# A decoder block on one core: x loaded right behind c, the first transfers in a fixed order, silu on c's row, and matmuls on zeros while TensorE waits

## The chip, the cores and the metric

The kernel runs on one core of a Trainium2 chip. The metric is the device time of one execution in microseconds (us), given as the median of the runs shown. Engines are named as in the profile: PE is TensorE's matmul, PEld its weight load, DVE is VectorE, ACT is ScalarE, POOL is GpSimd, and SP (SPq in the trace) is SyncE, which issues the DMAs.

## What is computed

The reference is one decoder block on x of shape (1, 1024, 1024) with a conditioning vector c of 1024 numbers. Cut to what the change touches:

```python
c_act = silu(c)
cond = c_act @ ada_w + ada_b          # six rows of 1024: shift1, scale1, gate1, shift2, ...
h = rmsnorm(x, norm1_g) * (1 + scale1) + shift1
z = h @ w_in + b_in                   # u, v, val, gate: 512 columns each
y_a = spatial_gating_mixer(gelu(u), gelu(v), ...)
y_b = conformer_conv_mixer(val, gate, ...)   # val * sigmoid(gate), causal conv of 31 taps, norm, silu
x = x + gate1 * (concat(rmsnorm(y_a), rmsnorm(y_b)) @ w_out)
h2 = rmsnorm(x, norm2_g) * (1 + scale2) + shift2
x = x + gate2 * ((silu(h2 @ w_g) * (h2 @ w_up)) @ w_ffn_out)
return rmsnorm(x) * norm_f_g * (1 + scale_f) + shift_f
```

## The kernel before

x lies transposed in `xs`, eight tiles of 128 features by 1024 tokens, and the block works on the tokens in two halves of 512. Every matrix product is done in three matmuls (`mm3`, L623 to L627, and `product`, L945): each operand is split into a high part (ACT, a copy to the reduced type) and a low part (DVE or POOL, a subtraction), and high times high (L625), low times high (L626) and high times low (L627) are summed in a bank.

The stage that the change touches is the first one.

- c's row is loaded (L540), then x's first half in eight transfers of 256 KB (L545) and `colt`, the small parameter columns (L546). Only "behind c" is laid down for them, not what may come between.
- L558 to L561: two matmuls spread c's row over 128 partitions (one per half of the row), and ACT's silu on each result gives `cact`. A one-column sqrt behind them (L564) makes ACT load the table for sqrt early.
- The first norm is `rstd` (L653): for each of the eight tiles, ACT squares it (L663) and four narrow matmuls (128x32 by 128x128) sum the squares over the partitions (L670); then sqrt (L673, ACT), reciprocal (L674, DVE), four wide matmuls that spread the result over the partitions (L676), and with `copy=True` a copy from the bank into `r_n` (L682, ACT).
- The loop over the eight tiles k (L740 to L754): two rows of the conditioning weights of 512 KB each are loaded into `ypad` (L576; four buffers, so two tiles k deep), DVE multiplies each with `cact` and sums (L581), which gives the column of scale1 and of shift1 for this k. ACT finishes these (L744, L745). The weights `wk` of this k are loaded (512 KB, L603) and split (L608 on ACT, L609 on DVE). x is multiplied by the norm (L747, DVE), modulated (L749 gives the high part of h, L750 the full value, both ACT), and L751 (DVE) gives h's low part. Then 24 matmuls of 128x512: eight units of `wk` (four groups j, value and gate each), three matmuls each, into eight banks, so all of PSUM is taken in this loop.
- Behind the loop come `glu` (L693), the projection of u (`pu`), the second half's norm, the convolution (`conv_pair`, L867, on ACT, POOL and for the most part DVE), the mixer and so on; the feed-forward stage fills the second half of the time.

What is written in program order is not the order on the engines. At the end `fix_order` (L473) takes all instructions, plans the whole program three times over with its own table of costs (`duration`, L126, and the class `Clock`, L317), forwards (`forward`, L376) and backwards (`backward`, L433), keeps the best plan, and lays each engine's order down by that plan, SP's included. The pairs in `edges` go into the plan as "later behind earlier" (L209); a context `issue_after` (L498) makes such pairs on one engine. Until now an edge between two DMAs meant "behind the end of the earlier". Tiles of one tag take their buffers in program order (`Slots`, L243); the tag `raw` has four buffers, which c's row, `wk` and most later weights share.

Of the kernel before, what the change touches and what calls it, by code (L numbers as in the profile page):

```python
# [13 lines left out]
P = 128  # L14
# [20 lines left out]
N_POOL_TAPS = (6, 6)  # L35

# [135 lines left out]
class Graph:  # L172


    def __init__(self, instructions, edges, stacked, reusing):
# [32 lines left out]
        by_name = {s.ins.name: s for s in self.steps}  # L208
        for later, earlier in edges:  # L209
            by_name[later].before.add(by_name[earlier].n)  # L210
# [165 lines left out]
def forward(g, rank):  # L376
# [25 lines left out]
    for _ in range(count):  # L402
# [21 lines left out]
        for n in s.after:  # L424
            need[n] -= 1
            same = g.steps[n].engine == e and not s.dma
            at[n] = max(at[n], (clock.free[e] if e == "PE" else end) if same else end + SIGNAL[e])
            if not need[n]:
                arrive(n)
# [3 lines left out]
def backward(g, rank, follows):  # L433
# [16 lines left out]
    for _ in range(count):  # L450
# [13 lines left out]
        for n in before[s.n]:  # L464
            need[n] -= 1
            other = g.steps[n].engine
            at[n] = max(at[n], begin + s.issue - (s.finish - s.issue) if other == e == "PE" else end + SIGNAL[other])
# [22 lines left out]
def block_kernel(ctx: ExitStack, tc: tile.TileContext, xT, c, ada, cols, vbias, bs, wsp,  # L490
# [52 lines left out]
    with issue_after(c_load):  # L543
        for k in range(KD):
            nc.sync.dma_start(xs[k][:, hs(0)], xT[k, :, hs(0)])  # L545
        nc.sync.dma_start(colt, cols)  # L546

# [8 lines left out]

    cact = const.tile([P, D], F32, name="cact")
    for h in range(2):  # L558
        cb = cv_bank(f"c{h}")
        PE.matmul(cb, ones[0:1].broadcast_to([1, P]), c_row[0:1, hs(h)], start=True, stop=True)  # L560
        silu = A.activation(cact[:, hs(h)], cb, AF.Silu).ins  # L561
# [39 lines left out]
    def weights(src, name, lo_eng, tag="w"):  # L601
        raw = sb.tile([P, 1024], F32, tag="raw", name=f"raw_{name}", bufs=N_RAW)
        nc.sync.dma_start(raw, src)  # L603
# [4 lines left out]
        A.activation(hi, raw, AF.Copy)  # L608
        lo_eng.tensor_tensor(lo, raw, hi.bitcast(F32), op=ALU.subtract)  # L609
# [123 lines left out]
    r1a_bank, r1a = rstd(x_half(0), D, "n1_0", (1,) * 8, None, True)  # L733
    h1 = [[None] * KD, [None] * KD]
    alloc = [cv_bank] * 2 + [gn_bank] * 2 + [mm_bank] * 3 + [nrm_bank]
    acc = {(j, vg): alloc[2 * j + vg](f"p{j}_{vg}") for j in range(4) for vg in range(2)}
    gain = const.tile([P, KD], F32, name="gain")
    V.scalar_tensor_tensor(gain, bcol(SCALE1, 0, KD), 1.0, colt[:, _OFF["norm1_g"]:_OFF["norm1_g"] + KD],
                           op0=ALU.add, op1=ALU.mult)
    for k in range(KD):  # L740
        for m, g in ((SCALE1, 0), (SHIFT1, 1)):
            ada_cols(m * 8 + k, dst=ypad[(2 * k + g) % 4][:, HALO:HALO + D])
        w_k = weights(wk[k], f"k{k}", V)
# [5 lines left out]
        A.activation(h[:, 0, :], t, AF.Identity, bias=ccol(SHIFT1, k), scale=ccol(SCALE1, k))  # L749
        A.activation(t, t, AF.Identity, bias=ccol(SHIFT1, k), scale=ccol(SCALE1, k))  # L750
        V.tensor_tensor(h[:, 1, :], t, h[:, 0, :].bitcast(F32), op=ALU.subtract)  # L751
        for j in range(4):
            for vg in range(2):
                mm3(acc[j, vg], unit(w_k, 4 * vg + j), full(h), k == 0, k == KD - 1)  # L754
# [688 lines left out]
```

## Time and profile before

| | |
|---|---|
| time, median of 3 runs | 990.24 us (989.9 to 991.04) |
| span of the profiled execution | 988.3 us; its whole time is not listed apart |
| instructions | 13193 |
| DVE, share of the span | 862.3 us, 87% |
| ACT, POOL | 474.2 us (48%), 399.5 us (40%) |
| bytes moved by DMA | 184.08 MB, mean 186 GB/s |

A profile row gives busy times of one execution. PE's share counts matmuls that overlap in the pipeline: one of 128x512 is shown with about 390 ns, and the next begins some 227 ns behind it at full clock. So the starts, not the durations, tell how fast PE works. Rows of the timeline give start, duration, engine, line, operation, output and inputs, and in brackets how long the engine had been idle and what ended that. Rows of the chain give start, duration, engine, tile and line of the work that the last instruction can be followed back to. Rows by stretch give, for each engine, busy time and instructions, then the granted clock, the DMA engines' busy share and GB/s.

### The profile page before, as it was taken

Reading aid. Unit: us, or ns where it says so; the run is one execution under the profiler, and the core shown is the slowest. Engines: PE = TensorE matmul, PEld = TensorE weight load, DVE = VectorE, ACT = ScalarE, POOL = GpSimd, SP = SyncE. Lnnn points to the kernel's source line nnn. Section 1 sums busy time; section 2 is a strip of 40 time slices with the busy share of each in tenths; the row PEclk is TensorE's granted clock in tenths of the full one; section 3 lists DMA queues with packets and bytes.
Section 4 is the critical chain, followed back from the end, with each engine's and each line's share of the span. In section 5 each row is a group of like instructions: output and inputs, shape, how many; then the busy total and the mean of one; then the engine's idle time right before and its main releaser. Section 6 shows DMA issues by size and latency. Waiting matters only on the chain.

```text
span 988.3 us, 13193 instructions
## 1 busy us (share of the span) xinstructions
PE 961.0 (97%) x4645; PEld 774.3 (78%) x4645; DVE 862.3 (87%) x1197; ACT 474.2 (48%) x750; POOL 399.5 (40%) x232
## 2 busy tenths in 40 slices
PE   6999999999999999999999999999999999999994
PEld 3887777778878778888888888888888887888873
DVE  4989999879999654799999999999779989869946
ACT  6778467553473563564323333323337437236416
POOL 0058879665554211574454544554443100000121
PEclk9999999999999999999999999999999999999997
DMA  9982451434465524864677677767659928315104
GB/s 328 333 308 83 139 173 53 170 107 128 149 227 178 160 80 166 261 230 149 222 239 243 218 240 254 256 220 228 221 178 298 325 83 260 126 36 179 33 1 170
DMA packets 72515, 184.08 MB, mean 186 GB/s; under 512 B 8065, under 2 KB 8321, under 8 KB 72450
## 3 DMA queue, kind: packets, MB, share of 16 engines
q1 hardware_dynamic: 72450, 183.25, 55.7%
q8 instruction: 36, 0.59, 0.3%
q14 instruction: 29, 0.24, 0.1%
HBM read 142.06 MB, written 41.16 MB: 185 GB/s over the span
## 4 chain that ended last, share of the span: by engine, by line
PE 81%; DVE 10%; ACT 4%; issue 2%; DMA 1%; POOL 1%; SPq 0%; ACTq 0%; DVEq 0%; POOLq 0%
PE B L950 28%; PE C L950 16%; PE ah L950 11%; DVE cv L888 4%; PE A L950 3%; PE po L625 3%; PE po L626 3%; PE po L627 3%; PE p L627 3%; PE p L625 3%; PE p L626 3%; PE pm L829 1%; PE gn L923 1%; DVE w_f L943 1%; DVE x L581 1%
## 5 line engine op out<-in xcount | busy, mean ns | idle before, releaser
L950 PE MATMUL B<-h,w_f 128*128 128x512 f32 x816 | 190.0, 390 | 1.1 <-DVE x L1169 1.0
L950 PEld LDWEIGHTS B<-h,w_f 128*128 128x128 f32 x816 | 152.8, 188 | 34.3 <-DVE x L1169 2.2
L888 DVE SCALAR_TENSOR_TENSOR cv<-ypad,colt,cv 128x512 f32<-128x512 f32 x216 | 146.3, 746 | 0.1
L950 PE MATMUL B<-fa,w_d 128*128 128x512 f32 x528 | 125.3, 390 | 0.5 <-DVE x L1302 0.5
L950 PE MATMUL C<-h,w_f 128*128 128x512 f32 x528 | 123.6, 389 | 0.0
L950 PEld LDWEIGHTS B<-fa,w_d 128*128 128x128 f32 x528 | 98.7, 188 | 21.9 <-DVE x L1302 1.0
L950 PEld LDWEIGHTS C<-h,w_f 128*128 128x128 f32 x528 | 99.1, 188 | 20.6
L950 PE MATMUL ah<-h,wh_a 128*128 128x512 f32 x320 | 100.8, 394 | 0.5 <-ACT sg L695 0.5
L1231 POOL TENSOR_TENSOR sq_nf<-sq_nf,sq_nf 128x512 f32<-128x512 f32 x9 | 12.4, 1374 | 178.3 <-ACT sq_nf L1226 178.3
L942 ACT ACTIVATE w_d<-raw_d 128x512 fp32r<-128x512 f32 (+1 forms) x72 | 42.0, 593 | 82.0 <-PE B L950 34.6
L609 POOL TENSOR_TENSOR wl_a<-raw_a,wh_a 128x1024 fp32r<-128x1024 f32 x20 | 49.3, 2464 | 72.3 <-ACT wh_a L608 62.2
L942 ACT ACTIVATE w_f<-raw_f 128x512 fp32r<-128x512 f32 x68 | 42.3, 628 | 74.3 <-PE B L950 41.6
L1192 POOL TENSOR_TENSOR x<-x,up 128x512 f32<-128x512 f32 x20 | 35.1, 1753 | 105.5 <-ACT x L1191 105.5
L950 PEld LDWEIGHTS ah<-h,wh_a 128*128 128x128 f32 x320 | 59.8, 188 | 14.9 <-issue 1.4
L943 DVE TENSOR_TENSOR w_f<-raw_f,w_f 128x512 fp32r<-128x512 f32 x68 | 65.6, 970 | 3.5 <-ACT w_f L942 3.4
L950 PE MATMUL C<-fa,w_d 128*128 128x512 f32 (+1 forms) x273 | 64.4, 384 | 0.2 <-DVE x L1302 0.2
L950 PE MATMUL ah<-h,wl_a 128*128 128x512 f32 x160 | 62.8, 394 | 0.0
L950 PEld LDWEIGHTS C<-fa,w_d 128*128 128x128 f32 x273 | 49.9, 188 | 10.8 <-issue 0.6
L1302 DVE SCALAR_TENSOR_TENSOR x<-B,cond,x 128x512 f32<-128x512 f32 x48 | 35.6, 743 | 23.2 <-PE B L950 23.2
L943 DVE TENSOR_TENSOR fa<-a,fa 128x512 fp32r<-128x512 f32 x77 | 53.3, 732 | 1.5 <-ACT fa L942 1.5
L942 ACT ACTIVATE fa<-a 128x512 fp32r<-128x512 f32 x77 | 46.2, 626 | 8.3 <-DMA a<-acts 5.2
L943 DVE TENSOR_TENSOR w_d<-raw_d,w_d 128x512 fp32r<-128x512 f32 (+1 forms) x72 | 46.6, 658 | 0.0
(236 smaller groups left out, 2115.0 us busy)
## 6 DMA issues: line engine op xcount, KB each, us to landing
acts<-x SPq DMA_DIRECT2D x77, 256.0 KB, 2.9
a<-acts SPq DMA_DIRECT2D x77, 256.0 KB, 4.3
raw_f<-wf SPq DMA_DIRECT2D x32, 512.0 KB, 4.5
ada<-ada SPq DMA_DIRECT2D x24, 512.0 KB, 3.4
x<-ada SPq DMA_DIRECT2D x24, 512.0 KB, 3.6
raw_a<-wf SPq DMA_DIRECT2D x20, 512.0 KB, 3.8
ahead<-ahead SPq DMA_DIRECT2D x40, 256.0 KB, 3.1
ypad<-ada SPq DMA_DIRECT2D x16, 512.0 KB, 5.3
```

The lines of the kernel that those rows point to most:

```text
L581: V.scalar_tensor_tensor(raw, raw, 1.0, cact, op0=ALU.mult, op1=ALU.mult, accum_out=cond[:, j:j + 1])
L609: lo_eng.tensor_tensor(lo, raw, hi.bitcast(F32), op=ALU.subtract)
L625: PE.matmul(acc, shi, mhi, start=start, stop=False)
L626: PE.matmul(acc, slo, mhi, start=False, stop=False)
L627: PE.matmul(acc, shi, mlo, start=False, stop=stop)
L888: V.scalar_tensor_tensor(accs[j], src, wc, accs[j], op0=ALU.mult, op1=ALU.add)
L942: A.activation(dst[:, 0, :], src, AF.Copy)
L943: lo_eng.tensor_tensor(dst[:, 1, :], src, dst[:, 0, :].bitcast(F32), op=ALU.subtract)
L950: last_mm = PE.matmul(bank[:, cols], s, m[:, cols], start=first and p == 0 and i == 0, stop=p == n - 1 and i == 2, skip_group_check=True)
L1192: G.tensor_tensor(g0, g0, up0, op=ALU.mult)
L1231: G.tensor_tensor(sums[half], sums[half], t, op=ALU.add)
L1302: V.scalar_tensor_tensor(xs[k][:, part], bank[:, cols], ccol(GATE2, k), xs[k][:, part], op0=ALU.mult, op1=ALU.add)
```

## The change

1. **Order of the first transfers.** `first_loads` holds the first ten DMAs (c, eight of x, `colt`), and edges put each behind the one before. `in_turn` appends the loads of the loop over k: scale row, shift row, weights, for k = 0 to 7. So nothing of the loop is issued ahead of x. `wk` of k = 0 is loaded and split in two parts of 512 columns.
2. **The planner.** An edge between two DMAs without another reason to wait is now a "turn": the later may be issued 0.44 us (the plan's figure) behind the earlier's issue, no longer behind its end.
3. **silu on c's row.** One silu of 1 x 1024 on ACT ahead of the two matmuls, and two copies from the banks to `cact` on DVE.
4. **The first norm** is written out in `first_rstd`: tiles 1 and 3 and half of tile 7 are squared on DVE. r's copy goes behind the high part of the first h. Of k = 0, the product with x reads the bank as before.
5. **Matmuls on zeros.** A tile `idle` of zeros (128x512, bf16) is multiplied into the bank of group 3's value, which the loop's first real matmul there overwrites: 3 ahead of c, 1 behind the sums of each of tiles 0 to 6, 4 behind tile 7's, 8 behind the matmuls that spread r; 22 in all. The banks of the loop are allocated when first used, this one at once.

```diff
+IDLE = (3, 1, 4, 8)
...
         for later, earlier in edges:
-            by_name[later].before.add(by_name[earlier].n)
+            a, b = by_name[later], by_name[earlier]
+            if a.dma and b.dma and b.n not in a.before:
+                self.turns.add((b.n, a.n))
+            a.before.add(b.n)
...
+            if (s.n, n) in g.turns:
+                at[n] = max(at[n], t + DMA_ISSUE)
...
+    first_loads = [i for i in nc.cur_bb.bb.instructions if "DMACopy" in type(i).__name__]
...
+    idle = front.tile([P, H], BF16, tag="vn", name="idle", bufs=4)
+    V.memset(idle, 0.0)
+    def keep_busy(n, after=None):
+        for _ in range(n):
+            ins = PE.matmul(idle_bank, idle[:, 0:P], idle, start=True, stop=True).ins
+            if after is not None:
+                edges.append((ins.name, after.name))
...
+    c_banks_0 = [cv_bank(f"c{h}") for h in range(2)]
+    idle_bank = first_bank(3, 0)
+    keep_busy(IDLE[0])
+    silu = A.activation(c_row[0:1, :], c_row[0:1, :], AF.Silu).ins
     for h in range(2):
-        cb = cv_bank(f"c{h}")
-        PE.matmul(cb, ones[0:1].broadcast_to([1, P]), c_row[0:1, hs(h)], start=True, stop=True)
-        silu = A.activation(cact[:, hs(h)], cb, AF.Silu).ins
+        PE.matmul(c_banks_0[h], ones[0:1].broadcast_to([1, P]), c_row[0:1, hs(h)], start=True, stop=True)
+        V.tensor_scalar(cact[:, hs(h)], c_banks_0[h], 1.0, None, op0=ALU.mult)
...
+        cuts = [slice(i * 1024 // parts, (i + 1) * 1024 // parts) for i in range(parts)]
+        for cut in cuts:
+            nc.sync.dma_start(raw[:, cut], src[:, cut])
...
+        for cut in cuts:
+            A.activation(hi[:, cut], raw[:, cut], AF.Copy)
+            lo_eng.tensor_tensor(lo[:, cut], raw[:, cut], hi[:, cut].bitcast(F32), op=ALU.subtract)
...
-    r1a_bank, r1a = rstd(x_half(0), D, "n1_0", (1,) * 8, None, True)
+    def first_rstd():
+        bank = nrm_bank("ssq_n1_0")
+        for k in range(KD):
+            src = xs[k][:, hs(0)]
+            t = tmp(f"sq_n1_0_{k}")
+            if k in (1, 3):
+                V.tensor_tensor(t, src, src, op=ALU.mult)
+            elif k == KD - 1:
+                A.activation(t[:, 0:256], src[:, 0:256], AF.Square)
+                V.tensor_tensor(t[:, 256:H], src[:, 256:H], src[:, 256:H], op=ALU.mult)
+            else:
+                A.activation(t, src, AF.Square)
+            for q in range(4):
+                mm = PE.matmul(bank[q * 32:(q + 1) * 32, 0:P], ones.broadcast_to([P, 32]),
+                               t[:, q * P:(q + 1) * P], start=k == 0, stop=k == KD - 1).ins
+            keep_busy(IDLE[2] if k == KD - 1 else IDLE[1], mm)
+        rt = sb.tile([P, P], F32, tag="rt", name="rt_n1_0", bufs=2)
+        A.activation(rt, bank[:, 0:P], AF.Sqrt, bias=epst, scale=1.0 / D)
+        V.reciprocal(rt, rt)
+        for q in range(4):
+            mm = PE.matmul(bank[:, q * P:(q + 1) * P], col("sel_tok", q).broadcast_to([P, P]),
+                           rt, start=True, stop=True).ins
+        keep_busy(IDLE[3], mm)
+        return bank
...
+    def in_turn(n):
+        for i in nc.cur_bb.bb.instructions[n:]:
+            if "DMACopy" in type(i).__name__:
+                edges.append((i.name, first_loads[-1].name))
+                first_loads.append(i)
+    for a, b in zip(first_loads[1:], first_loads):
+        edges.append((a.name, b.name))
     for k in range(KD):
-        for m, g in ((SCALE1, 0), (SHIFT1, 1)):
-            ada_cols(m * 8 + k, dst=ypad[(2 * k + g) % 4][:, HALO:HALO + D])
-        w_k = weights(wk[k], f"k{k}", V)
+        n_before = len(nc.cur_bb.bb.instructions)
+        ada_cols(SCALE1 * 8 + k, dst=ypad[2 * k % 4][:, HALO:HALO + D])
+        ada_cols(SHIFT1 * 8 + k, dst=ypad[(2 * k + 1) % 4][:, HALO:HALO + D])
+        w_k = weights(wk[k], f"k{k}", V, parts=2 if k == 0 else 1)
+        in_turn(n_before)
...
-        A.activation(h[:, 0, :], t, AF.Identity, bias=ccol(SHIFT1, k), scale=ccol(SCALE1, k))
+        h_hi = A.activation(h[:, 0, :], t, AF.Identity, bias=ccol(SHIFT1, k), scale=ccol(SCALE1, k)).ins
+        if k == 0:
+            with issue_after(h_hi):
+                A.activation(r1a, r1a_bank, AF.Copy)
```

More of the change, by code (lines that the diff above doesn't have):

```diff
@@ L466, in backward @@
             other = g.steps[n].engine
+            if (n, s.n) in g.turns:
+                at[n] = max(at[n], begin + DMA_ISSUE)
+                if not need[n]:
+                    heapq.heappush(waiting[other], (at[n], n))
+                continue
             at[n] = max(at[n], begin + s.issue - (s.finish - s.issue) if other == e == "PE" else end + SIGNAL[other])
@@ L753, in block_kernel @@
             for vg in range(2):
[L754 removed]
+                mm3(first_bank(j, vg), unit(w_k, 4 * vg + j), full(h), k == 0, k == KD - 1)
     first_phase_loaded = ada_dma[SHIFT1 * 8 + KD - 1].ins
```

19 lines of the change are left out of this document (12 added, 7 removed).

## The prediction

> **What bounds the kernel now.** I read the page first: its head, the engines' shares and the chain that ended last.
>
> ```profile
> span 988.3 us, 13193 instructions
> ...
> PE 961.0 (97%) x4645; PEld 774.3 (78%) x4645; DVE 862.3 (87%) x1197; ACT 474.2 (48%) x750; POOL 399.5 (40%) x232
> ...
> PE 81%; DVE 10%; ACT 4%; issue 2%; DMA 1%; POOL 1%; SPq 0%; ACTq 0%; DVEq 0%; POOLq 0%
> ```
>
> TensorE carries the end: 97% busy, 81% of the chain. An average hides where the missing time lies, so next the busy times by stretch (after the engine's own time: PE, PEld, DVE, ACT, POOL).
>
> ```profile
> 0.00:20.00 20.00, 10.96 (x77) 5.06 (x78) 6.93 (x13) 12.21 (x21) 0.49 (x8) 1.00 0.90 334
> ```
>
> ```profile
> 20.00:65.00 45.00, 45.00 (x190) 36.95 (x189) 41.07 (x57) 30.78 (x46) 7.99 (x3) 1.00 0.92 315
> 65.00:100.00 35.00, 34.37 (x205) 26.66 (x204) 33.64 (x49) 30.08 (x47) 27.78 (x20) 1.00 0.42 147
> 100.00:160.00 60.00, 59.90 (x338) 47.15 (x337) 59.69 (x93) 37.03 (x58) 50.94 (x26) 1.00 0.42 134
> ...
> 400.00:700.00 300.00, 298.97 (x1343) 246.30 (x1335) 295.80 (x362) 112.08 (x183) 149.99 (x88) 1.00 0.71 231
> ```
>
> PE misses 9 us of the first 20, and almost nothing later: from 20 to 160 it is idle for 0.7 us, from 400 to 700 for 1.0. So what PE wins in the first 20 us reaches the end unless something makes it wait later. The timeline of those 20 us shows the chain that holds it up:
>
> ```profile
> 1.22 0.82 SPq L576 DMA_DIRECT2D ypad<-ada  x2
> 2.09 4.54 SPq L545 DMA_DIRECT2D x<-xT  x8
> ...
> 2.40 3.75 PE L560 MATMUL c<-c_row,ones 1*128 1x512 f32 x4 [2.40 <-DMA c_row<-c]
> ...
> 6.98 0.63 ACT L663 ACTIVATE sq_n<-x 128x512 f32<-128x512 f32 x1 [0.20 <-DMA x<-xT]
> 7.63 1.28 ACT L564 ACT_TABLE_LOAD   x1
> ...
> 8.93 0.20 ACT L564 ACTIVATE warm<-epst 128x1 f32<-128x1 f32 x1
> 9.03 3.92 ACT L663 ACTIVATE sq_n<-x 128x512 f32<-128x512 f32 x7
> ...
> 9.70 3.96 PE L670 MATMUL ssq_n<-sq_n,ones 128*32 128x128 f32 x56 [1.38 <-ACT sq_n L663]
> ...
> 13.72 0.37 ACT L673 ACTIVATE rt_n<-ssq_n,epst 128x128 f32<-128x128 f32 x1 [0.22 <-PE ssq_n L670]
> 13.99 1.05 ACT L608 ACTIVATE wh_k<-raw_k 128x1024 fp32r<-128x1024 f32 x1
> 14.12 0.95 DVE L674 RECIPROCAL rt_n<-rt_n 128x128 f32<-128x128 f32 x1 [1.36 <-ACT rt_n L673]
> ...
> 15.13 2.08 PE L676 MATMUL ssq_n<-rt_n,colt 128*128 128x128 f32 x8 [1.48 <-DVE rt_n L674]
> 17.25 0.60 ACT L682 ACTIVATE r_n<-ssq_n 128x512 f32<-128x512 f32 x1 [2.21 <-PE ssq_n L676]
> 17.88 0.69 DVE L747 TENSOR_TENSOR t_h<-x,ssq_n 128x512 f32<-128x512 f32 x1 [1.58 <-ACT r_n L682]
> 18.60 0.81 ACT L749 ACTIVATE h<-t_h,cond 128x512 fp32r<-128x512 f32 x1 [0.76 <-DVE t_h L747]
> ...
> 19.47 0.80 PE L625 MATMUL p<-h,wh_k 128*128 128x512 f32 x1 [2.26 <-ACT h L749]
> ```
>
> Two conditioning rows (1 MB) go ahead of x, so x's first tile lands at 6.98; ACT loads the sqrt table and squares until 12.95; sums, sqrt, reciprocal, the spreading matmuls, r's copy, product and modulation follow one another, and the first real matmul starts at 19.47. Then it is slow:
>
> ```profile
> 24.10 0.43 PE p L626
> ...
> 24.83 0.23 PE p L625
> ```
>
> ```profile
> 65.48 0.39 PE L625 MATMUL pu<-h,wh_u 128*128 128x512 f32 x1
> ...
> 86.88 1.16 PE L676 MATMUL ssq_n<-rt_n,colt 128*128 128x128 f32 x8
> ```
>
> Up to 24.1 one matmul takes 0.43 us, from 24.83 on 0.23 (65.48 is where the loop's 192 matmuls are over; at 0.2267 they need 43.5). (65.48 - 24.83) / 0.2267 is 179 matmuls, so 13 ran in the slow 5.36 us, which at the fast pitch are 2.95: the slow start costs **2.4 us**. The granted clock reads 1.00 there, so the pitch is the evidence. The same eight spreading matmuls took 2.08 us at 15.13 and 1.16 at 86.88: PE was at half pace then, too, although it had been busy with the narrow sums.
>
> **The change part by part.** *Loads.* Stretches of the DMA engines:
>
> ```profile
> 2.70:5.40 2.70, 2.70 (x4) 0.83 (x3) 0.00 (x0) 0.60 (x1) 0.00 (x0) 1.00 0.98 362
> 5.40:11.60 6.20, 3.30 (x41) 1.01 (x40) 2.38 (x4) 5.19 (x9) 0.00 (x0) 1.00 1.01 347
> 14.00:20.00 6.00, 2.61 (x9) 2.28 (x10) 4.29 (x6) 3.00 (x5) 0.00 (x0) 1.00 1.02 409
> ```
>
> ```profile
> SPq L546 <- DMA x<-xT: 0.3, 1, 0.3
> ```
>
> Before 5.4 the 1 MB of conditioning passes, then x's 2.1 MB at 347 GB/s in 6.05 us; tile 0's bytes are through at 6.15 and it lands at 6.96, 0.8 later. With x first the same starts at 2.7: tile 0 lands at 4.2, tile 7 at 9.6. Behind it `colt` (138.5 KB, 0.4), then 512 KB each at 409 GB/s, 1.28 us: the scale row lands at 11.2, the shift row at 12.5, the two parts of `wk` (256 KB, 0.76 each at x's rate) at 13.3 and 14.05, k = 1's three at 15.3, 16.6 and 17.9. SP issues in this order; it already waits for earlier landings (row above), and its queue holds nothing else that is due then. The conditioning lands 4 us later than before; what covers this is that it is wanted only with r.
>
> *silu and squares.* c is there at 2.4. silu on 1x1024 is bounded by ACT's rows of that width (`wh_k`, 1.05) and of half of it (0.63); I take 1.05, the nearest: 3.45. The sqrt table (1.28) and the one-column sqrt (0.2) end at 4.95, when tile 0 has been there for 0.7. ACT then has five and a half squares of 0.56 and DVE two and a half of about 0.69 (its 128x512 rows), all faster than x lands (0.76 a tile). So the last half square ends 0.4 behind tile 7: 10.0, against 12.95. The two copies to `cact` on DVE (0.61 to 0.75 each, nearest its product row's 0.69) lie where DVE is idle before, in front of the first product at 12; the zero tile's fill too, whatever it costs below that.
>
> *Chain.* Sums 0.7 behind the last square, as before (12.95 to 13.66): 10.75. sqrt 0.4: 11.15. Reciprocal: 12.1. Spreading 1.16 to 2.08: 13.3 to 14.25. r's copy (0.63) leaves the path; ACT does it behind h, and r is next wanted by k = 1's product four us later. Now **DVE is late next**. Its rows:
>
> ```profile
> 18.48 1.22 DVE L581 SCALAR_TENSOR_TENSOR ypad<-ypad,cact 128x1024 f32<-128x1024 f32 x1
> 19.63 1.22 DVE L581 SCALAR_TENSOR_TENSOR ypad<-ypad,cact 128x1024 f32<-128x1024 f32 x1
> ...
> 28.89 0.68 DVE L751 TENSOR_TENSOR h<-t_h,h 128x512 fp32r<-128x512 f32 x1
> ...
> 33.52 0.68 DVE L751 TENSOR_TENSOR h<-t_h,h 128x512 fp32r<-128x512 f32 x1
> ```
>
> The conditioning products (a new one can start every 1.15) run from 12.1 to 14.4, then the product with x to 15.1, h to 15.95, with signals of 0.03 to 0.06 each step: the first real matmul at **16.2**. If DVE takes the product with x straight behind the spreading, 14.9; that is the lower end. From there DVE needs 4.63 us for one k (28.89 to 33.52), PE 5.44, so PE is fed: k = 1's h is ready at about 20.7, PE is through k = 0 at 21.6. A landing 0.9 later than worked out would show as a wait there.
>
> *Zeros.* No bf16 matmul is in the trace; between nothing and twice the loop's pitch, I take that pitch, 0.23 fast and 0.43 slow, the nearest row of that width. Ahead of c and between the sums the zeros delay nothing if PE is fast by then; the last eight fill 1.8 of the 2.9 us between the spreading and 16.2 (at twice the pitch 3.6, and the start is 16.9). If PE is slow they cost, see the second rival.
>
> When does PE get fast? It is busy with few breaks from 3.45: c's matmuls 3.75, then sums and zeros. The trace before has 5.0 us of unbroken 128x512 matmuls ahead of the change of pitch, and it shows narrow sums (9.7 to 13.7) that brought none. The Trainium skill, TensorE: Matmul & The Clock Gate, Part 1, has half rate as the default and full rate after one busy window of about 3.4 us that runs freely. By that rule a busy time from 3.45 opens the clock by 10.3 at the latest; that the narrow sums did not open it speaks against counting every matmul as busy. By the rule the start stays 16.2 (16.8 at worst), by the strict reading of the rows it is the second rival.
>
> *Sum.* Start 19.47 - 16.2 = 3.3, pace 2.4: **5.7 us**. The loop ends at 59.7 instead of 65.48. DVE's added 3.2 us (squares, copies) lie in its 13 idle us before 20. The span would be 982.6. The median of the runs is 990.24, 1.9 above the one profiled span; taken off there: **984.5**.
>
> All engines' orders are planned anew, so every later wait may shift by some tenths in either direction. I put that at nothing, within 1 us each way.
>
> **The rivals.** *A, DVE in the convolution holds the time.* The chain runs on DVE before the mixer's matmuls at 145.6:
>
> ```profile
> 95.46 13.91 DVE cv L888 x22
> ...
> 145.63 1.97 PE gn L923 x32
> ```
>
> From 20 to 160 DVE is busy 134.4 of 140. Work up to 160 is then 6.9 + 134.4 + 3.2 = 144.5; 4.6 of it is over at 12.1 (fills, copies, squares, gain, reciprocal). The other 139.9 with the same 5.6 of waits end at 157.6: only 2.4 earlier, time 987.8. Without the waits it would be 8.0 earlier. For A: that chain. Against: part of those waits are for PE's loop, which ends earlier, and PE has other matmuls at hand.
>
> *B, the zeros do not open the clock.* At half pace c's matmuls end at 7.2, eight sums of 0.56 (3.96 / 7) and seven zeros of 0.43 at 14.7, the reciprocal at 16.1, the spreading at 18.2. If the clock opens half-way through the last eight zeros, they end at 20.8. Loop end 20.8 + 43.5 = 64.3, gain 1.2: 989.0. The change would then not do what it says; the zeros would cost what the early x brings.
>
> *C, slower: DVE overruns in the feed-forward stage.* From 400 to 700 DVE has 4.2 us left of 300, and PE lives on its splits. DVE's time there depends on what lies beside it:
>
> ```profile
> L581 DVE SCALAR_TENSOR_TENSOR x<-x,cact x24: 1209/1215/2322, 477.9 to 691.6; 128x1024 f32<-128x1024 f32 x24
> ```
>
> ```profile
> L581 DVE SCALAR_TENSOR_TENSOR x<-x,cact 128x1024 f32<-128x1024 f32 x24 | 36.0, 1502 | 0.0
> ```
>
> The same product takes 1.21 to 2.32 us, on average 1.50. If the new order put all 24 at 2.32, DVE would need 19.7 more; 4.2 is free, PE loses 15.5, less 5.7: 1000.0. It decides from 9.9 us more DVE time on (parity); at three quarters, 14.8, the time is 995.1. Against it: only the first stage's costs change, and the order there need not.
>
> **How the numbers follow.** Forecast 0.58 (own range 983 to 986), A 0.15, B 0.15, C 0.12. This kernel's measurement can tell about 0.2%, 2 us, from no change. Faster: the forecast, A and a little of B, 0.77; same: the rest of B, 0.12; slower: C, 0.11. The low end is the start at 14.9 (gain 7.0) with some tenths of luck, 982.8; the high end takes in A and B, 989.2; C is left out.
>
> **What would show it.** Right: tile 0's square starts near 5, the last ends near 10, the first real matmul of the loop starts near 16 with pitch 0.23 at once, `pu` begins near 59.7, and PE has under 2 us of new waits behind it. Wrong: the spreading matmuls still take 2.08 and the zeros stand between h and the first real matmul (B); `pu` early but the mixer's matmuls near 145 not earlier by more than 3 (A); DVE's products above 1.5 us in the feed-forward stage and PE waiting for w_f (C). If tile 7 lands later than 10.5, my rate for x was wrong, and the start moves with it.

## The result, and the profile after

The changed kernel takes **992.58 us** (median of 20 runs, 989.08 to 995.05), the kernel before in the same comparison 990.4 (20 runs, 989.25 to 991.8): a ratio of 1.0022, 95% interval 1.0014 to 1.003. It is 2.2 us slower where 5.7 us less were forecast, and lies 3.4 us above the predicted range. Its profiled execution took 994.9 (span 993.2), so it stands 2.3 above the median: what is read from it is a slow example of its kind.

The head of its page, the shares, and the chain that ended last:

```profile
span 993.2 us, 13233 instructions
...
PE 968.5 (98%) x4667; PEld 775.4 (78%) x4667; DVE 860.1 (87%) x1204; ACT 473.6 (48%) x748; POOL 392.9 (40%) x232
...
PE 73%; DVE 15%; DMA 5%; issue 2%; ACT 2%; SPq 1%; POOL 1%; ACTq 0%; DVEq 0%; POOLq 0%
```

TensorE's share of the chain fell from 81% to 73%, DVE's rose from 10% to 15% and the DMAs' from 1% to 5%: other things than PE now end waits. The start of its timeline:

```profile
4.00 0.63 ACT L782 ACTIVATE sq_n<-x 128x512 f32<-128x512 f32 x1 [0.61 <-DMA x<-xT]
...
9.32 2.08 ACT L782 ACTIVATE sq_n<-x 128x512 f32<-128x512 f32 x3 [2.65 <-DMA x<-xT]
...
11.43 0.42 ACT L779 ACTIVATE sq_n<-x 128x256 f32<-128x256 f32 x1
...
12.03 0.61 PE L584 MATMUL p<-idle 128*128 128x512 bf16 x1
12.57 0.66 PE L784 MATMUL ssq_n<-sq_n,ones 128*32 128x128 f32 x8
13.16 3.17 PE L584 MATMUL p<-idle 128*128 128x512 bf16 x7
...
13.69 0.95 DVE L789 RECIPROCAL rt_n<-rt_n 128x128 f32<-128x128 f32 x1 [1.74 <-ACT rt_n L788]
14.56 1.16 DVE L615 SCALAR_TENSOR_TENSOR ypad<-ypad,cact 128x1024 f32<-128x1024 f32 x1
...
15.65 1.22 DVE L615 SCALAR_TENSOR_TENSOR ypad<-ypad,cact 128x1024 f32<-128x1024 f32 x1
...
16.12 1.10 PE L791 MATMUL ssq_n<-rt_n,colt 128*128 128x128 f32 x8
...
17.06 2.54 PE L584 MATMUL p<-idle 128*128 128x512 bf16 x11
...
17.26 0.69 DVE L820 TENSOR_TENSOR t_h<-x,ssq_n 128x512 f32<-128x512 f32 x1 [0.38 <-PE ssq_n L791]
...
18.04 0.81 ACT L822 ACTIVATE h<-t_h,cond 128x512 fp32r<-128x512 f32 x1 [0.31 <-DVE t_h L820]
...
19.24 0.58 PE L662 MATMUL p<-h,wh_k 128*128 128x512 f32 x1
```

x's first tile is there at 4.00, close to the 4.2 worked out, but the fifth only at 9.32, and the last half tile is squared at 11.43. The program has eleven zero matmuls behind the tiles' sums, one for each of seven tiles and four behind the last. One of the eleven came to stand ahead of the last sums (12.03) and seven in one heap at 13.16, ahead of the matmuls that spread r: the reciprocal is done at 14.64, the spreading starts at 16.12. Eleven more, the remaining three and the last eight, fill PE up to 19.2, while h is ready at 18.85. The first real matmul starts at 19.24, 0.23 earlier than before.

By stretch (PE, PEld, DVE, ACT, POOL; granted clock, DMA share, GB/s):

```profile
3.00:11.40 8.40, 7.55 (x52) 2.39 (x52) 2.58 (x4) 4.92 (x8) 0.00 (x0) 1.00 0.90 315
...
20.00:65.00 45.00, 43.72 (x193) 35.86 (x192) 39.00 (x57) 30.67 (x48) 5.45 (x2) 1.00 0.86 287
65.00:100.00 35.00, 32.85 (x194) 25.93 (x193) 30.15 (x45) 29.47 (x43) 28.62 (x19) 0.95 0.57 195
80.00:85.00 5.00, 5.00 (x35) 3.48 (x28) 4.64 (x8) 4.44 (x7) 5.00 (x4) 0.66 0.54 169
```

PE's waits from 58 to 90 and from 400 to 700, each for the kernel before and then after (total, times, longest):

```profile
PE ssq_n L670 <- ACT sq_n L663: 0.4, 1, 0.4
```

```profile
PE ssq_n L707 <- ACT sq_n L700: 2.1, 1, 2.1
PE pu L662 <- ACT sg L732: 1.3, 1, 1.3
```

```profile
PE B L950 <- DVE x L1169: 1.0, 2, 0.7
```

```profile
PE B L1026 <- DVE x L1245: 2.9, 3, 1.5
```

The loop runs at full pace from its first matmul, and its last one starts at 62.8 (before: 65.3). So 2.5 us were won there. Then PE waits 1.3 us for the sigmoids that free the banks for `pu` and 2.1 us for the squares of the second half's norm, and behind this second wait the clock falls: 0.66 over 80 to 85 is 5.00 x 0.34 / 0.5 = 3.4 us at half pace, 1.7 us lost. With 3.0 us more of waits and 1.7 of clock, the 2.5 us have become a loss of some 2.2 by 85. The feed-forward stage adds 1.9 us of waits for `x` (2.9 against 1.0).

### The profile page after: what moved, and what is told of

Its sections match the earlier page's. It is cut to its first block, busy times and chain, and to the rows that moved or that the text cites. A ratio compares the mean times of both kernels' runs of the same rounds, so it can differ in the third digit from the quotient of the medians.

```text
span 993.2 us, 13233 instructions
## 1 busy us (share of the span) xinstructions
PE 968.5 (98%) x4667; PEld 775.4 (78%) x4667; DVE 860.1 (87%) x1204; ACT 473.6 (48%) x748; POOL 392.9 (40%) x232
## 4 chain that ended last, share of the span: by engine, by line
PE 73%; DVE 15%; DMA 5%; issue 2%; ACT 2%; SPq 1%; POOL 1%; ACTq 0%; DVEq 0%; POOLq 0%
PE B L1026 23%; PE C L1026 13%; PE ah L1026 11%; PE po L662 3%; PE po L663 3%; PE po L664 3%; PE A L1026 3%; DVE cv L964 2%; DVE w_f L1019 2%; PE p L662 2%; PE p L663 2%; PE p L664 2%; DVE x L615 1%; PE v L662 1%; DMA a<-acts 1%
## 5 line engine op out<-in xcount | busy, mean ns | idle before, releaser
L1026 PE MATMUL ah<-h,wl_a 128*128 128x512 f32 x160 | 62.8, 394 | 0.0
L1019 DVE TENSOR_TENSOR w_d<-raw_d,w_d 128x512 fp32r<-128x512 f32 (+1 forms) x72 | 48.6, 685 | 0.4 <-ACT w_d L1018 0.4
```

What stands on the lines that cost most here:

```text
L1019: lo_eng.tensor_tensor(dst[:, 1, :], src, dst[:, 0, :].bitcast(F32), op=ALU.subtract)
L1026: last_mm = PE.matmul(bank[:, cols], s, m[:, cols], start=first and p == 0 and i == 0, stop=p == n - 1 and i == 2, skip_group_check=True)
```

## The experiments

Each kernel was timed beside the kernel before, whose median there was 989.96 to 990.67; the ratio is to that. Three landmarks are read from each profile: where PE starts the projection of u (`pu`) and DVE the glu, both behind the first loop, and where PE starts the mixer's first `gn` matmul. Kernels called "pinned" have, behind the plan's time 53.5, the kernel before's own order on every engine. So their `gn` stands in the same place of the same order as in the kernel before, and its time tells what was won or lost up to there.

| kernel | median (n) | ratio, 95% interval | `pu` | glu | `gn` |
|---|---|---|---|---|---|
| before, profiled execution | | | 65.48 | 63.11 | 138.76 |
| the changed kernel | 992.58 (20) | 1.0022, 1.0014 to 1.003 | 64.44 | 63.27 | |
| after_again | 993.25 (7) | 1.0033, 1.0023 to 1.0044 | 63.41 | 62.24 | |
| p1_before_order | 992.78 (7) | 1.0028, 1.0017 to 1.0039 | 65.03 | 66.27 | 140.03 |
| p2_ffn_before_order | 990.36 (12) | 0.9993, 0.9981 to 1.0006 | 62.46 | 61.29 | |
| p3_before_ffn_after_order | 991.82 (9) | 1.0018, 1.0009 to 1.0028 | 64.94 | 62.57 | 138.23 |
| q1_bank | 991.27 (11) | 1.0009, 1.0 to 1.0018 | 64.08 | 67.20 | 142.78 |
| q2_no_zeros | 991.42 (11) | 1.0005, 0.9996 to 1.0015 | 64.77 | 65.04 | 140.76 |
| q3_zeros_in_place | 989.63 (11) | 0.9993, 0.9984 to 1.0002 | 64.42 | 64.71 | 138.36 |
| q4_before_bank_first | 990.25 (11) | 1.0, 0.9992 to 1.0009 | 66.11 | 63.73 | 139.41 |
| r1_rows | 990.14 (11) | 0.9997, 0.9988 to 1.0006 | 64.64 | 64.91 | 138.27 |
| r2_rows_ahead | 989.26 (12) | 0.9993, 0.9984 to 1.0003 | 64.48 | 63.92 | 140.05 |
| r3_x_first | 989.86 (11) | 1.0, 0.9991 to 1.0009 | 64.79 | 62.42 | 138.07 |
| r4_before_rows | 990.73 (11) | 1.0, 0.9992 to 1.0009 | 64.90 | 62.52 | 138.19 |
| s1_x_early | 993.58 (5) | 1.0032, 1.002 to 1.0044 | 66.17 | 67.94 | 142.17 |
| s2_before_x_early | 991.47 (12) | 1.0014, 1.0004 to 1.0023 | 65.62 | 65.89 | 139.26 |
| s3_more_dve | 990.87 (11) | 1.0005, 0.9996 to 1.0013 | 64.80 | 64.62 | 138.13 |
| s5_product_behind_glu | 992.78 (11) | 1.0028, 1.0019 to 1.0037 | 65.77 | 66.40 | 141.38 |
| t1_zeros_alone | 991.12 (12) | 1.001, 1.0 to 1.0021 | 67.82 | 65.45 | 141.06 |
| t2_zeros_x_first | 991.16 (12) | 1.0001, 0.9992 to 1.001 | 65.64 | 65.89 | 139.36 |

The landmarks belong to one execution each and shift by a microsecond or two from one to the next (q4, which computes just as the kernel before, has its `gn` 0.65 later). So a verdict rests on the ratio, and the landmarks say where to look.

### Is it the new order of the engines?

The first theory: the engines' orders, planned anew, give back what the start wins. p1 takes the changed kernel with the old orders from 53.5 on, p2 only from 338 on (the feed-forward stage), and p3 puts the new order of that stage into the kernel before. after_again is the changed kernel once more.

```diff
+    pin(best[1], g.steps)
     for steps in best[1].values():
         for earlier
```

> The changed kernel once more, as the control on the same chip and for a second profile. Every theory: 1.002 times the kernel before. Theory 1 (the re-made order of the rest costs): the second profile too shows the loop over k done 2 to 3 us earlier than before, and 3 to 4 us lost again between 460 and 640 us, where PE waits for DVE. Theory 2 (the first stage's own side effects cost, and what follows is only shifted in time): the loss between 460 and 640 differs from profile to profile by more than 2 us.

> The changed kernel, but everything behind the first half or so of the loop over k (the plan's time 53.5) keeps the order that the kernel before has on every engine. Theory 1 (the re-made order of the rest costs): faster than before, by the 2.5 us that the loop ends earlier in the first profile, less the 1.3 us that the first projection of u waits for the bank that the zeros took: 1 to 2.5 us faster, ratio 0.9975 to 0.999. Theory 2 (the first stage's own side effects, the bank and the clock, cost): still slower than before by 1 us or more, ratio over 1.001.

> The changed kernel, but from the plan's time 338 on (the last of the block ahead of the feed-forward stage, and that stage) every engine keeps the order of the kernel before. Theory 1: the 3 to 4 us that were lost in the feed-forward stage come back, so the time is 2 to 3.5 us under the changed kernel's, ratio to before 0.999 to 1.0015. Theory 2: no change against the changed kernel, ratio 1.002.

> The kernel before, with nothing of the change, but from the plan's time 338 on with the order that the changed kernel has on every engine. Theory 1: the loss comes with this order alone, 2 to 4 us slower than before, ratio 1.002 to 1.004. Theory 2: the order makes no difference, ratio 0.9995 to 1.0005.

The changed kernel came out slower again. With the feed-forward stage's old order (p2) it is level with the kernel before: 2.9 us are that order's by the medians (993.25 - 990.36), 4.0 by the ratios. Put into the kernel before, the same order alone costs 1.9 us (991.82 against 989.96, whose ratio's interval lies above 1). PE's waits for `x` from 400 to 700, in p2 and in p3:

```profile
PE B L1141 <- DVE x L1360: 0.5, 1, 0.5
```

```profile
PE B L1065 <- DVE x L1284: 1.8, 3, 1.0
```

So the order of that stage is shown to cost 2 to 4 us. But it is not all: p2 still has nothing of the 5.7 us, and p1, whose orders are old from 53.5 on, missed its expectation altogether. Its place of loss is the one that the profile after showed. PE's waits from 58 to 90, then DVE's rows there, then PE's stretch 60 to 70 in p1:

```profile
PE pu L829 <- ACT sg L899: 2.3, 1, 2.3
PE ssq_n L874 <- ACT sq_n L867: 0.4, 1, 0.4
```

```profile
65.11 1.23 DVE L782 SCALAR_TENSOR_TENSOR ada<-ada,cact 128x1024 f32<-128x1024 f32 x1 [3.25 <-DMA ada<-ada]
...
66.27 2.72 DVE L901 SCALAR_TENSOR_TENSOR ypad<-p,colt,sg 128x512 f32<-128x512 f32 x4
```

```profile
60.00:70.00 10.00, 7.67 (x27) 5.82 (x27) 6.72 (x11) 7.42 (x11) 4.81 (x3) 0.83 0.79 283
```

The glu stands on DVE behind a conditioning product, and DVE stood 3.25 us for that product's row. It starts the glu 3.2 us later than in the kernel before, although PE's loop was done earlier.

### Is it the zeros, or their bank?

The second theory: the zeros are written into the bank of group 3's value, which the glu empties last, and so hold up what comes behind. q1 is p1 with the zeros in a bank of group 1; q2 is p1 without zeros; q3 is q1 with each zero tied between its tile's sums and the next; q4 is the kernel before with group 3's bank allocated first.

```diff
-    idle_bank = first_bank(3, 0)
+    idle_bank = first_bank(1, 0)
...
-IDLE = (3, 1, 4, 8)
+IDLE = (3, 1, 3, 5)
...
+                if q == 0 and zero is not None:
+                    edges.append((mm.name, zero.name))
-            keep_busy(IDLE[2] if k == KD - 1 else IDLE[1], mm)
+            zero = keep_busy(IDLE[2] if k == KD - 1 else IDLE[1], mm)
```

> The changed kernel with the order of before behind the loop (as in p1_before_order), and with one more edit: the zeros go into a bank of the tag gn (group 1's value) instead of group 3's, so the first bank of the tag mm is group 2's again, as before the change. Theory 1 (the bank that the zeros take is the one that u's first projection gets, and it is the last to come free): the wait of 2.3 us ahead of pu goes, the half clock of 3.4 us behind it too, and the 3 us of the loop reach the end: 2.5 to 4 us faster than before, ratio 0.996 to 0.9975. Theory 2 (PE would wait there whatever the bank, since the activation behind the loop comes no earlier): pu still waits 2 us, ratio 1.002 to 1.003.

> As p1_before_order, without any matmul on zeros (and so with the banks in their old turn). Theory 1: the seven zeros that stood between the sums and the spreading matmuls (1.4 us) and the last ones ahead of h (0.4 us) are gone, the first real matmul starts near 17.5, but at half pace, which costs up to 2.4 us; pu does not wait. The loop ends 1 to 3 us earlier than before: ratio 0.997 to 0.999. Theory 2 (the zeros are what brings the gain of the loop): the loop ends no earlier than before, ratio 0.9995 to 1.0005.

> As q1_bank, with the zeros tied in place: each group of sums stays behind the zero of the group before it, so none slides to the end, and 3 instead of 4 behind the last sums, 5 instead of 8 behind the spreading. Theory 1: the spreading matmuls start when the reciprocal is done (near 14.8 instead of 16.1), the first real matmul near 18.4 instead of 19.2, at full pace: 0.5 to 1 us faster than q1_bank, ratio to before 0.995 to 0.997. Theory 2 (what stands ahead of the spreading is hidden, the conditioning products on DVE hold h back): within 0.3 us of q1_bank.

> The kernel before, with its own order behind the loop, and one edit: group 3's value bank is allocated ahead of the other seven. No zeros, no other part of the change. Theory 1: u's first projection gets the bank that comes free last and waits 2 us for it, with the half clock behind it 3 to 4 us slower than before: ratio 1.002 to 1.004. Theory 2: no difference, ratio 0.9995 to 1.0005.

q4 shows that in the kernel before the bank alone costs nothing. In q1 the ratio falls from p1's 1.0028 to 1.0009, so the bank may be a part of it there, though the two intervals still touch. It is not the whole: the wait for `pu` is gone, but it has moved. PE's wait and its stretch 80 to 90:

```profile
PE ssq_n L874 <- ACT sq_n L867: 4.1, 1, 4.1
```

```profile
80.00:90.00 10.00, 5.85 (x47) 3.87 (x38) 10.00 (x16) 8.03 (x13) 9.36 (x7) 0.83 0.34 110
```

The same happens in q2 without any zeros (waits of 0.9 and 1.5 us and 0.83 over 80 to 90). With the zeros kept in place, q3, the waits are small and the clock stays open:

```profile
PE ssq_n L875 <- ACT sq_n L868: 0.9, 1, 0.9
PE pu L830 <- ACT sg L900: 0.6, 1, 0.6
```

q3 is level with the kernel before and 1.6 us below q1 (the two intervals overlap a little). The gain is not at the start. There q3 is later than q1 (19.49) and than its own expectation (18.4):

```profile
19.99 0.50 PE L830 MATMUL p<-h,wh_k 128*128 128x512 f32 x1 [1.56 <-ACT h L992]
```

The zeros that are tied between the sums hold these up: until 11.8 a tile's sums and its zero take 1.12 us together.

### Is it the row buffers, or x?

In the changed kernel k = 0's two products run at 14.56 to 16.8 instead of 6.8 to 9.2, and the buffers of the conditioning rows come free that much later. The third theory made this the cause. r1 is q3 with eight row buffers instead of four, r2 is q3 with k = 0's rows loaded ahead of x again, r3 is the kernel before with x first alone, r4 the kernel before with eight row buffers. All are pinned.

```diff
+    row = [y[:, HALO:HALO + D] for y in ypad] + [f32_tile(f"row{i}") for i in range(4)]
...
-        ada_cols(SCALE1 * 8 + k, dst=ypad[2 * k % 4][:, HALO:HALO + D])
-        ada_cols(SHIFT1 * 8 + k, dst=ypad[(2 * k + 1) % 4][:, HALO:HALO + D])
+        ada_cols(SCALE1 * 8 + k, dst=row[2 * k % 8])
+        ada_cols(SHIFT1 * 8 + k, dst=row[(2 * k + 1) % 8])
```

> The version with the zeros in place (q3), and four more buffers for the conditioning rows of the first stage (8 instead of 4), so that a row's load need not wait for the product of the row two steps before. Theory 3 (with x ahead of the rows, k=0's products run late, the row buffers come free late, all later loads of the first stage come 2 to 4 us later, and the matmuls that start earlier wait for them at 62 to 85 us): the last wk load is issued at 38 us or earlier (39.9 to 43.7 without the buffers), the waits of TensorE between 60 and 90 us are under 1 us in sum, no half clock there; 987 to 988.5 us, 0.997 to 0.9985 of before. Theory 4 (between 62 and 85 us ACT and DVE work at their own pace, whatever the loads do): the loads come earlier, but the waits at 62 to 85 us stay, and the time is that of q3, 989.5 to 990.5.

> The version with the zeros in place (q3), but the two conditioning rows of k=0 are loaded ahead of x again, as in the kernel before; all else as in q3. Theory 3: k=0's products run before x has landed, k=2's rows are issued at 11 to 12 us and the last wk load at about 40; x's last tile lands some 3 us later, so the first real matmul comes 2 to 3 us later than in q3, nearly as late as before, and nothing waits at 62 to 85 us: 989 to 990.5. Theory 4 (the loads do not matter): the later start is lost whole, 990.5 to 991.5.

> The kernel before with one part of the change alone: the first transfers in the new fixed order (c, x, cols, then the rows and weights in turn), with the order of before on every engine behind the plan's time 53.5. Theory 3: TensorE's first real matmul comes 1 to 2 us earlier, the rows of k=2 are issued at 15 to 16 us, the last wk load 2 to 4 us later than before's 40.4, and what the start gains is lost by 90 us with some more: 990 to 992. Theory 4: the earlier start stays in part, 988.5 to 989.5.

> The kernel before with the four more row buffers alone, its own order on every engine behind the plan's time 53.5. Theory 3: in the kernel before TensorE does not wait for the loads of the first stage, so the buffers bring 0 to 1 us: 989.3 to 990.5. If the buffers alone bring over 1.5 us, they are a gain of their own, and what r1 shows is to be read against this run.

r1's loads do run ahead: the last of `wk` and the first of `wu` are out by 38.4 (after: 45.5). Yet its time is that of q3, and DVE ends the loop no sooner. The last low part of `wk` on DVE, in the kernel before, after, and in r1:

```profile
49.77 1.22 DVE L609 TENSOR_TENSOR wl_k<-raw_k,wh_k 128x1024 fp32r<-128x1024 f32 x1
```

```profile
51.84 1.22 DVE L646 TENSOR_TENSOR wl_k<-raw_k,wh_k 128x1024 fp32r<-128x1024 f32 x1
```

```profile
51.40 1.23 DVE L814 TENSOR_TENSOR wl_k<-raw_k,wh_k 128x1024 fp32r<-128x1024 f32 x1 [0.36 <-ACT wh_k L813]
```

So the buffers are not it; the third theory falls, and its rival (behind the loop ACT, DVE and POOL keep their own pace) got r1 right. r2 and r3 came out level, each within its interval of no change: whether the rows or x go first does not show in the time. That fits neither theory well: r2's 989.26 lies in the range of the third one, r3's 989.86 in neither's. r4 brings nothing, as expected.

### Is it DVE, later by the moved products?

The fifth theory: k = 0's two products (2.3 us) have moved from DVE's idle time into a stretch in which it has none; DVE ends the loop 1.2 to 2.1 us later (rows above; in q3 the row stands at 51.02), its next product falls beside POOL's split of `wu`, the fourth `wu` load gets its buffer late, x's second half stands behind that in SP's queue, and the squares and the glu are late. s3 gives the kernel before 1.15 us more DVE work in the loop, an unused product; s1 is q3 with x's second half loaded early, s2 the same in the kernel before, s5 is s1 with the product in front of the glu put behind it.

```diff
+        if k == 2:
+            more = f32_tile("more")
+            work = V.scalar_tensor_tensor(more, cact, 1.0, cact, op0=ALU.mult, op1=ALU.mult).ins
+            edges.append((work.name, th0.name))
```

```diff
+    order["SP"] = rest[:at] + move + rest[at:]
...
+    dve.remove(row)
+    dve.insert(dve.index(glu) + 1, row)
```

> The version with the zeros in place (q3), with the eight loads of x's second half moved ahead in SP's queue to right behind the bias of v (issued at 42 to 46 us in place of 53 and 60 to 63). Theory 5 (x's second half stands behind a wu load whose buffer DVE frees late): ACT's squares at 65 to 69 us no longer wait for x, the convolution chain behind them runs 0.5 to 1 us earlier, TensorE's wait for the squares at 79 us is under 0.5 us; the wait for the glu (0.6) stays; 988.5 to 989.3. Theory 4 (ACT, DVE and POOL set the pace whatever the loads do): the time of q3, 989.5 to 990.5.

> The kernel before with x's second half loaded right behind the bias of v, its own order otherwise. By every theory the kernel before does not wait for x's second half after 62 us, so this changes under 0.5 us: 989.5 to 990.8.

> The kernel before with one more instruction on DVE between k=2 and k=3 of the first loop (a product of 128x1024 into a spare tile, 1.15 us, its result unused), its own order otherwise. Theory 5: DVE, which has no idle time there, ends the loop 1.15 us later; the fourth wu load and with it x's second half are issued 1.5 to 3.5 us later; TensorE is not late at the loop's end, but waits 1 us or more at 79 to 80 us, and where the wait passes 1 to 1.5 us the clock falls to half for 3.4 us: 991.5 to 993. Theory 4 or any other in which DVE's slack of 12 us in the loop covers it: 990.0 to 990.8.

> s1 with one more move: on DVE the third conditioning product behind the loop (3.3 us at 61.4 in q3) stands behind the four glu products in place of ahead of them. Theory 5: the glu follows ACT's sigmoids at once, TensorE's waits at 64 and 79 us are both under 0.5 us, the loop's gain stays to the end, no half clock: 987 to 988.5. Theory 4: no better than s1.

s3 shows the first links. The next conditioning product on DVE takes 3.4 us instead of 1.2, and six tiles of x's second half are issued at 60.55 instead of 58.73, as late as in q3 (the product in s3, then SP's row in s3 and in the kernel before):

```profile
52.28 3.44 DVE L748 SCALAR_TENSOR_TENSOR ada<-ada,cact 128x1024 f32<-128x1024 f32 x1
```

```profile
60.55 3.04 SPq L1149 DMA_DIRECT2D x<-xT  x6
```

```profile
58.73 3.04 SPq L974 DMA_DIRECT2D x<-xT  x6
```

But its time is 1.0005 (0.9996 to 1.0013), and PE waits 0.5 us there. The theory had said 991.5 to 993: it fails for the kernel before, whose PE comes to the glu at about the time when a late DVE does (glu at 64.62, `pu` at 64.80). The same lateness meets PE in q3, where the loop ends at 63.8.

The chain of work in q3's trace runs over these links: DVE's product at 56.21 (3.44 us), the `wu` load issued at 59.66, x's second half from 60.52 on, ACT's square of it at 68.04. But r2's chain does the same (56.24, 59.70, 60.56, 68.22), and in r2 the two products of k = 0 run at 10.55 and 11.69, well ahead of the reciprocal at 16.61. So the links are there, but the moved products are not shown to be what makes them late.

s1 and s5 were to take the last links away and made things worse. SP's eight transfers of x, DVE's next two rows, and the wait of PE for h in s1:

```profile
42.89 8.48 SPq L1235 DMA_DIRECT2D x<-xT  x8
```

```profile
58.08 1.23 DVE L798 SCALAR_TENSOR_TENSOR ada<-ada,cact 128x1024 f32<-128x1024 f32 x1 [5.78 <-DMA ada<-ada]
...
59.23 0.69 DVE L1012 TENSOR_TENSOR h<-t_h,h 128x512 fp32r<-128x512 f32 x1
```

```profile
PE p L847 <- DVE h L1012: 1.1, 1, 1.1
```

SP took 8.5 us to issue them, the conditioning row behind them came late, DVE stood 5.8 us for it, and h's low part, which the loop's last matmuls need, stood behind. In the kernel before the same move (s2) costs 0.14%, where under 0.5 us had been expected. The load queue has no free place here: a transfer drawn forward pushes another back, and DVE's order turns that into a wait.

### Can the start's gain be kept with DVE's work as before?

t1 adds the zeros alone to the kernel before, t2 the zeros and x first; squares, silu and r's copy stay as they were. Both are pinned. In t2 the two products of k = 0 still run late, at 13.19 and 15.27, because their rows come behind x; so only t1 leaves them in DVE's idle time.

```diff
+            if name == "n1_0":
+                zero = keep_busy(IDLE[2] if g == len(groups) - 1 else IDLE[1], mm)
```

> The kernel before with the zeros alone (3 at the start, 1 behind each tile's sums, 3 and 5 behind the last tile's and the spreading, in a bank of group 1, tied in their places), x, silu and r's copy as before. Theory 5: the clock is open from about 12 us on without a break, the first real matmul comes at 19 to 19.5 as before, the loop ends 2 to 2.6 us earlier than before's 65.5, DVE is no later than before, and 0.5 to 2 us of it stay to the end: 988.3 to 989.8. Theory 4 (the stage of 62 to 85 us, the chain glu, convolution, squares, ends when ACT, DVE and POOL let it, whatever TensorE does): nothing stays, 990 to 991, and a wait of 1.5 us or more at 64 or 79 us takes the gain.

> The kernel before with the zeros in place and the first transfers in the new order (t1 and r3 together); squares, silu and r's copy as before. Theory 5: the first real matmul comes at 18 to 19.5, at full pace, the loop ends at 62.5 to 63.5, and as DVE has the work of the kernel before, 1 to 2 us stay: 988 to 989.5, the fastest of all versions. Theory 4: 990 to 991, the gain taken by waits at 64 or 79 us.

Neither brought anything. In t1 the zeros stand in the way, as in the prediction's second rival:

```profile
9.88 0.66 PE L854 MATMUL ssq_n<-sq_n,ones 128*32 128x128 f32 x8 [0.84 <-ACT sq_n L847]
...
10.46 0.61 PE L734 MATMUL p<-idle 128*128 128x512 bf16 x1
...
11.00 0.66 PE L854 MATMUL ssq_n<-sq_n,ones 128*32 128x128 f32 x8
...
17.14 0.95 DVE L862 RECIPROCAL rt_n<-rt_n 128x128 f32<-128x128 f32 x1 [0.80 <-ACT rt_n L861]
```

Sums and one zero take 1.12 us per tile as long as the clock is closed, ACT's squares 0.56. PE falls behind, and the reciprocal starts at 17.14 (before: 14.12). In t2 the loop starts at 19.01 at full pace and its last matmul starts at 63.1, and then

```profile
PE pu L821 <- ACT sg L898: 2.1, 1, 2.1
```

takes all of it. In none of the pinned kernels does `gn` start ahead of 138.07 (r3); before, it started at 138.76. **No version beat the kernel before**; the lowest ratios (p2, q3, r2: 0.9993) have intervals that hold 1.

## Why the prediction was wrong, point by point

- **"tile 7 lands at 9.6", the rate of x: wrong by 1.8 us.** The last half square started at 11.43, as soon as tile 7 was there, 1.8 later than worked out. From the first tile (4.00) to the fifth (9.32) four tiles of 256 KB took 5.3 us, and 2.7 of it lay between the third and the fourth. From 4.0 to 9.4 the engines moved 274 GB/s in place of 347 (315 over the row's 3.0 to 11.4), nearly all in packets of 2 KB, the length of x's rows; the conditioning rows behind x, of 4 KB, took nothing from it. The kernel before has two rates for x, too: 270 GB/s from 6 to 8 us and 389 from 8 to 11. The 347 was an average over both; what makes the slow stretch stays open. The prediction had named this as what would move the start.
- **"Ahead of c and between the sums the zeros delay nothing": wrong by 1.3 us.** One zero delayed the last sums by 0.5 (12.03). Seven held up the spreading by 1.5 (14.64 to 16.12), but DVE had the conditioning products until 16.87 and waited only 0.4 for the bank (17.26). The last zeros delayed the first real matmul by 0.4. The plan had let them drift from their tiles: an edge said only "behind". With the 1.8 us of x this is the whole miss of the start, 19.24 in place of 16.2, so of the term 3.3 us only 0.2 came. Other executions with this first stage started at 17.84 (p2) to 19.02 (after_again).
- **The pace, 2.4 us: right.** The first real matmuls follow at 0.23, and the loop ended 2.5 us earlier, 0.2 of it by the start.
- **"The conditioning lands 4 us later than before; what covers this is that it is wanted only with r", cost nothing: DVE paid for it, but a cost in time is not shown.** It is wanted by DVE first. The two products moved behind the reciprocal, where DVE has nothing free (from 20 to 52 the trace of the kernel before names no wait of DVE): DVE ends the loop 2.1 us later. The prediction saw that DVE needs 4.63 us per k against PE's 5.44 and took this as enough; it did not ask what is queued behind DVE's part of the loop when PE gets there sooner. But the glu starts only 0.16 later than before, 1.15 us more on DVE (s3) cost nothing in the kernel before, and with the products early again (r2) the time is q3's.
- **"What PE wins in the first 20 us reaches the end unless something makes it wait later": this is where the mechanism failed.** From 62 to 85 PE's new waits and the half clock took 4.7 us in the profiled execution. That PE missed only 0.7 us between 20 and 160 was read as "PE is the bound". The chain that ended last says otherwise; in the kernel before it leaves PE behind the loop:

```profile
64.06 0.24 PE p L627
64.32 0.70 ACT sg L695
...
74.95 5.66 POOL s L883 x3
...
81.26 1.66 ACT sq_n L663 x3
```

From there it goes on to the convolution on DVE and comes back to PE only with `gn` at 145.63, a row that the prediction shows. For 81 us PE is busy with matmuls that the chain does not wait for. An earlier loop helps only by way of the sigmoids (`sg`) of its last group, and only until something else on that chain is late. In q3 it is x's second half and POOL, on which ACT waits:

```profile
67.29 1.39 ACT L868 ACTIVATE sq_n<-x 128x512 f32<-128x512 f32 x2 [0.87 <-DMA x<-xT]
...
80.24 0.72 ACT L1128 ACTIVATE cp<-ypad,colt 128x512 f32<-128x512 f32 x1 [1.49 <-POOL s L1129]
80.87 1.66 ACT L868 ACTIVATE sq_n<-x 128x512 f32<-128x512 f32 x3
```

The last three squares, which PE waits for, stand on ACT behind a copy for the convolution, and this waits for POOL: 1.49 us here, 1.50 in the kernel before, 1.23 in the changed kernel. q3's loop ends 1.8 us earlier than before, its last squares start 0.4 earlier (80.87 against 81.26), and so does `gn`.

- **"All engines' orders are planned anew ... I put that at nothing, within 1 us each way": wrong by 1.9 us (p3) to 2.9 (p2).** It is the place of the third rival, at a fifth of its price, by waits of PE for `x`.

The first rival (DVE in the convolution holds the time) names a stretch of this chain, and its sign came in q3: `pu` 1.1 us earlier, `gn` 0.4. But its price, 987.8, still allowed a gain of 2.4, and ACT and POOL ahead of DVE were not in it. The second's zeros in the way did happen, though the clock opened. Three parts make up the 8.1 us between forecast and median: 3.1 at the start, 2 to 4 by the order of the feed-forward stage, and the rest, 1 to 3, between 62 and 85.

What stays open: which of the things behind the loop (the row for the product, `wu` for ACT, x's second half) would have to come earlier for PE's gain to last. Single ones were freed (r1, s1, s5) and another took their place; freeing all at once was not tried, nor an order in which ACT's last squares do not stand behind the copy that waits for POOL.

## What to carry to other kernels

An engine that is nearly always busy need not be the only bound: before pricing a gain on it, follow the chain that ended last through the stages behind the change, see where it leaves that engine, and count only what the engine would find ready when it comes there sooner. Work that is moved from an engine's idle time into a stretch without any makes that engine late (here 2.1 us for 2.3 us of work), even if its result is wanted later. And where a planner orders the whole program, a local edit is also a new order everywhere: pin the rest when the edit is to be judged, and give the order's scatter (here 2 to 4 us) a place in the sum.

## What the runs showed of the hardware

- After a stall of PE the clock can fall to half for 3.4 us: 0.66 over five microseconds in the changed kernel, 0.83 over ten in after_again, p1, q1, q2, r2, s1 and t1 (0.88 in p2), with longest waits of 1.2 to 4.1 us ahead of it. Behind 0.9 us (q3) it stayed open, but so it did behind 2.1 us in t2 and 1.9 in s5. A short wait can cost 1.7 us more than itself; what decides was not settled. The Trainium skill, TensorE: Matmul & The Clock Gate, Why this matters for your kernels, asks for no gaps of PE above about 3 us; in these runs shorter ones did it, and the measurement decides.
- Zero matmuls among the narrow ones open the clock before the first real matmul. Between the sums they did so in q3 and t2: eight sums take 0.66 us at first, 0.42 from 11.84 (q3) and 9.70 (t2) on. In the changed kernel the heap did it: the spreading behind it took 1.10 us, 2.08 before. Without zeros (q2) the granted clock still reads 0.88 over 20 to 30 us.
- A product of 128x1024 on DVE takes 1.2 us alone and up to 3.4 us while POOL splits `wu` (s3). The Trainium skill, SBUF — State Buffer, Who interferes with whom, has the two engines share a port that one of them holds for its whole instruction; the 3.4 us fit a wait for POOL's 2.4 to 2.8 and the 1.2 of the product's own.
